# A two-layer decoder step: the sums of weights of the seven-product blocks made by adding transfers and VectorE, and the middle down products added up by transfers

## The chip, the cores and the metric

The kernel runs on one core of one Trainium2 chip. The metric is the time of one execution on the device, in microseconds (us). Before the change three runs gave 1215.65, 1221.56 and 1222.04 us, a median of 1221.56 us. The profile comes from one further execution of the same program.

## The reference, cut to what matters

One inference step runs a prompt of 512 tokens and 8 x 4 sample tokens, 544 rows in all, through two layers of width 1024. Layer 0 mixes tokens by causal pooling, layer 1 by a gated linear recurrence (HGRN2). Behind each mixer stands a gated ConvFFN, and the change lies in these two:

```python
def conv_ffn(h, ctx, w_up, conv_w, conv_b, w_down):
    L = h.shape[1]
    u = h @ w_up
    full = jnp.concatenate([ctx.astype(u.dtype), u], axis=1)
    c = conv_b + sum(full[:, j:j + L] * conv_w[j] for j in range(CONV_W))
    gate, val = jnp.split(c, 2, axis=-1)
    y = (jax.nn.gelu(gate, approximate=True) * val) @ w_down
    return y, full[:, -(CONV_W - 1):]
```

`w_up` is 1024 x 5632 (2816 gate and 2816 value columns), `w_down` 2816 x 1024, all float32.

## The kernel before, in words

**Layout.** Activations lie transposed: 128 channels on the partitions, 544 tokens along the free dimension. Each float32 operand of a large product is split into a rounded part and a remainder (`wh` and `wl` for weights, `h` and `l` for activations), and each product is three matmuls: `wh` by `h`, `wh` by `l`, `wl` by `h`. For a chunk of 128 x 512 weights ScalarE makes `wh` by copying, VectorE makes `wl` by subtracting (`ensure_units`). Ten buffers each for `wh` and `wl` let this run up to nine units ahead of TensorE (`ahead_units`).

**The ConvFFN (`ffn`).** The 2816 hidden channels are 22 pairs of one gate and one value block of 128. They come in five parts of 6, 4, 4, 3 and 5 pairs (`PARTS`). The down product of a part is eight blocks (`down(pi, o)`); those of part pi stand between the up products of part pi + 1 in the order of the table `MIX`, and the eight of the last part come at the end. `do_down` takes each result from its PSUM bank (`ps`) into the sum `m` (`mtile`): part 0 is copied by ScalarE, each later part is added by one VectorE instruction, `m<-m,ps`.

**Seven products instead of eight.** Pairs 0 to 5 are computed plainly. From pair 6 on, 16 pairs a layer, the gate and the value block are one 2 x 2 block product with seven half-size products in place of eight (`seven(j)`): the four halves of the two weight blocks and the two halves of the tokens are combined by sums and differences. The activations' sums are made once a layer in `operands(k, out)`, for k = 0 to 3, by four GpSimd subtractions of 128 x 272 each (tile `hold`, and `t`). The weights' sums are made for each pair in `seventh(i, q)`, q being the product: two loads of 512 KB fill two of the three `raw` buffers, three GpSimd additions of 128 x 512 follow, into a tile of its own (`sums`), into half of a `raw` buffer, and into a third tile (`fst`), and a fourth comes before the last product. A pair then takes 7 x 12 matmuls of 272 columns into three of the four PSUM banks called `pa`. ScalarE and VectorE combine the banks into `u`, and `finish` does the convolution: per block one ScalarE instruction (`t<-t,prm`), two VectorE instructions that multiply and add, SCALAR_TENSOR_TENSOR `t<-t,prm` 128x560, then for the gate a GELU on ScalarE, and for the pair the product `y` and its split into two parts for the down product.

**What sets the order.** Nearly every instruction is recorded by `Plan` and emitted by `Plan.emit`, a list scheduler that simulates the engines with the costs of `Plan.cost` and buffer release; the engines then run strictly in the emitted order. So a changed cost can move instructions anywhere in the program. Because a helper emits everything, all lines in the profile are L312, and tiles are what tells the groups apart.

**Names in the profile.** `raw`, `t`: loaded weights; `wup`, `wdn`: up and down weights in memory; `fst`: a tile that holds the convolution's saved rows and, behind them, a weight sum; `prm`: parameters; `op`, `k`, `xl`: split activations. The seven-product stages last from about 130 to 410 us in layer 0 and from about 880 to 1150 us in layer 1; `operands` runs at 80 to 130 and 830 to 880 us.

Of the kernel before, what the change touches and what calls it, by code (L numbers as in the profile page):

```python
# [17 lines left out]
P = 128  # L18
# [58 lines left out]
class Plan:  # L77
# [85 lines left out]
    @staticmethod  # L163
    def cost(eng, name, args, kw):
        out = args[0]
        n = 1
        for v in out.shape[1:]:
            n *= v
        if eng == "PE":
            f32 = str(args[1].dtype).endswith("float32")  # L170
            m = 1
            for v in args[1].shape[1:]:
                m *= v
            if name == "transpose":
                return 0.11
            if f32 and out.shape[0] <= 32 and args[1].shape[0] >= 96:
                return max(n / 2400 + 0.01, 0.0018 * m)
            return max(4 * n, 4 * min(m, 128)) / 2400 + 0.005 if f32 else n / 2400 + 0.003
        if name == "dma_start":
            return 0.475 if eng == "SP" else 1.04  # L180
        ins = [a for a in list(args[1:]) + list(kw.values()) if hasattr(a, "shape")]
        cols = sum(all(v == 1 for v in a.shape[1:]) for a in ins) if n > 1 else 0
        psum = any(str(getattr(a, "space", "")).endswith("PSUM") for a in ins)
        if eng == "ACT":
            return (0.0515 if psum else 0.0935) + n / 1200 + 0.0935 * cols
        if eng == "DVE":
            if name == "memset":
                return 0.01 + n / 960
            return 0.069 + n / (1920 if name == "tensor_scalar" and not psum else 960) + 0.06 * cols
        return 0.13 + n / 475  # L190

    def emit(self):
# [10 lines left out]
        dma = lambda o: 2.0 + int(np.prod(o[3][0].shape)) * 4 / 359e3  # L203
# [52 lines left out]
        for _ in range(n):  # L256
# [31 lines left out]
            if o[2] == "dma_start":  # L288
                st = max(at + o[7] + 0.65, dma_free)
                dma_free = st + dma(o) - 2.0  # L290
                end[i] = dma_free + 0.91
            else:
                end[i] = free[e]
# [52 lines left out]
def trunk_step(ctx: ExitStack, tc: _tile.TileContext, xT, xp, xs, spool, s0, fctx, par, gb0, cst, bands,  # L346
# [92 lines left out]
    sums, mine = {}, {}  # L439
# [39 lines left out]
    def seventh(i, q):  # L479


        H = 4 * P
        if q == 0:
            raws[i] = A_, B_ = [wp.tile([P, KT * P], F32, tag="raw", name="raw") for _ in range(2)]
            for t, src in zip((A_, B_), stream[i][0]):
                SP.dma_start(t, src)

            mine[i] = dict(sums) or {q: tt((P, H)) for q in range(2)}
            POOL.tensor_tensor(mine[i][0], A_[:, 0:H], B_[:, 0:H], op=ALU.add)
            POOL.tensor_tensor(B_[:, 0:H], B_[:, 0:H], B_[:, H:2 * H], op=ALU.add)  # L490
            POOL.tensor_tensor(mine[i][1], B_[:, 0:H], A_[:, 0:H], op=ALU.add)
        A_, B_ = raws[i]
        if q == 6:
            POOL.tensor_tensor(A_[:, H:2 * H], A_[:, H:2 * H], mine[i][1], op=ALU.add)
        return (mine[i][1], A_[:, 0:H], mine[i][0], B_[:, 0:H], A_[:, H:2 * H], B_[:, H:2 * H], A_[:, H:2 * H])[q]

# [415 lines left out]
    def ffn(li, XH, XL, res, enter, mtag, leave, n_ahead, homes, hv=HV):  # L912
# [70 lines left out]
        def do_down(pi, o, src, sl):  # L983
            if o == 0 and pi == LP and acc[0] is None:
                acc[0] = tt()
            if sl is None:
# [22 lines left out]
        def operands(k, out):  # L1009
# [22 lines left out]
        def operand(q, k):  # L1032

            t, c = ((out["a", k], 1), (out["a", k], 0), (out["w", k], 0), (out["w", k], 1), (out["z", k], 0), (out["s", k // 2], k % 2),
                    (out["z", k], 1))[q]
            return t[0][:, U[c]], t[1][:, U[c]]

        def seven(j):
            i = up_i[li, j]
            banks = [ps1()[:, 0:HT] for _ in range(3)]  # L1040
# [13 lines left out]
            Y, X, Z = banks  # L1054
            c, t = w[:, U[0]], w[:, U[1]]
            after = (lambda: ACT.activation(c, Y, AF.Identity),
                     lambda: DVE.tensor_tensor(t, c, X, op=ALU.subtract),
                     lambda: DVE.tensor_tensor(c, t, Z, op=ALU.add),
                     lambda: second(1, ALU.subtract, c, Y),
                     lambda: ACT.activation(u_of(0)[0][:, 2:2 + HT], X, AF.Identity),  # L1060
                     lambda: DVE.tensor_tensor(u_of(1)[0][:, 2:2 + HT], c, Z, op=ALU.add),
                     lambda: second(0, ALU.subtract, Y, t))
            for q, (o, more) in enumerate(((Y, 0), (X, 0), (Z, 0), (Y, 0), (X, 1), (Z, 0), (Y, 1))):
# [31 lines left out]
        def up(j):  # L1095
# [3 lines left out]
            for b in (j, NPAIR + j):  # L1099
# [3 lines left out]
                u, us = new_u(b)  # L1103
# [641 lines left out]
```

## Time and profile before

| What | Value |
|---|---|
| Runs | 1215.65, 1221.56, 1222.04 us, median 1221.56 |
| Profiled execution, its own time | 1218.57 us |
| Its span in the trace | 1216.7 us, 1.9 us less than its time |
| Granted TensorE clock over the span | 0.981 |
| TensorE busy | 1157.7 us (95%), 9892 matmuls |
| VectorE busy | 963.7 us (79%) |
| ScalarE busy | 632.7 us (52%) |
| GpSimd busy | 475.1 us (39%) |
| DMA | 134.04 MB, mean 110 GB/s |

A row of the groups gives line, engine, operation, written tile <- read tiles, shapes and count, then busy time and mean duration of one, then the idle time just before these instructions and what ended it. A row of the windows gives, for a stretch of the span, the busy time of each engine, the granted clock and the mean busy share of the 16 DMA engines. In a timeline row the first two numbers are start and duration; a bracket at the end is the engine's idle time before it and what ended that. DMA-issuing instructions on GpSimd do not count as busy.

### The profile page before, as it was taken

How to read it: one execution, taken by the hardware profiler on the slowest of the kernel's cores; microseconds unless marked ns; L12 is line 12 of the kernel's file. 1: busy time of each engine (PE TensorE's matmuls, PEld its weight loads, DVE VectorE, ACT ScalarE, POOL GpSimd, SP SyncE). 2: the span in 40 equal slices, each digit the busy share in tenths (PEclk: the TensorE clock that was granted, in tenths of full speed). 3: DMA queues.
4: the chain of work that ended last, by engine and by line, in shares of the span. 5: the costliest groups of instructions: out<-in, count | busy, mean ns of one | idle time of the engine just before them, and what ended most of it. 6: DMA issues, size and time to landing. Idle time of an engine off the chain costs nothing.

```text
span 1216.7 us, 25725 instructions
## 1 busy us (share of the span) xinstructions
PE 1157.7 (95%) x9892; PEld 1116.1 (92%) x9892; DVE 963.7 (79%) x2075; ACT 632.7 (52%) x1343; POOL 475.1 (39%) x709
## 2 busy tenths in 40 slices
PE   8999898999999999999999999999899999999895
PEld 7799898998999997999999999999899899998895
DVE  6788776888988877588778985577976998888866
ACT  4665555444444466556555554545545544444552
POOL 3547535354454233111111130427625446355413
PEclk9999999999999999999999999999899999999998
DMA  9883232221321376423232223457141232223232
GB/s 322 188 206 73 61 109 88 88 87 61 113 96 65 110 247 142 105 82 108 92 105 84 83 98 117 119 141 157 40 139 71 71 104 96 78 83 96 63 142 74
DMA packets 55243, 134.04 MB, mean 110 GB/s; under 512 B 6730, under 2 KB 13258, under 8 KB 55112
## 3 DMA queue, kind: packets, MB, share of 16 engines
q1 hardware_dynamic: 37168, 95.90, 23.4%
q0 software_dynamic: 17808, 36.44, 13.0%
q8 instruction: 78, 1.28, 0.4%
q14 instruction: 45, 0.37, 0.1%
q10 hardware_dynamic: 144, 0.05, 0.0%
HBM read 119.96 MB, written 12.77 MB: 109 GB/s over the span
## 4 chain that ended last, share of the span: by engine, by line
PE 58%; DVE 23%; issue 7%; ACT 6%; POOL 4%; DMA 2%; DVEq 0%; SPq 0%; ACTq 0%; POOLq 0%
PE ps L312 30%; PE pa L312 27%; DVE t L312 13%; DVE wl L312 5%; ACT t L312 3%; DVE m L312 2%; ACT wh L312 2%; PE pr L312 2%; POOL raw L312 1%; POOL fst L312 1%; DMA t<-bands 1%; DVE k L312 1%; DVE op L312 1%; POOL wh L312 0%; DMA k<-wup 0%
## 5 line engine op out<-in xcount | busy, mean ns | idle before, releaser
L312 PE MATMUL pa<-op,wh 128*128 128x272 f32 x1152 | 268.8, 298 | 23.6 <-ACT t L312 15.6
L312 ACT ACTIVATE wh<-raw 128x512 fp32r<-128x512 f32 (+2 forms) x294 | 172.7, 597 | 168.6 <-PE ps L312 68.0
L312 PE MATMUL ps<-t,wh 128*128 128x272 f32 x1248 | 241.3, 291 | 6.1 <-ACT t L312 4.2
L312 DVE TENSOR_TENSOR wl<-raw,wh 128x512 fp32r<-128x512 f32 (+2 forms) x294 | 199.5, 691 | 59.4 <-ACT wh L312 53.1
L312 PEld LDWEIGHTS pa<-op,wh 128*128 128x128 f32 x1152 | 200.3, 195 | 29.5 <-ACT t L312 18.9
L312 PE MATMUL pa<-op,wl 128*128 128x272 f32 x768 | 226.3, 295 | 0.9 <-DVE wl L312 0.9
L312 DVE SCALAR_TENSOR_TENSOR t<-t,prm 128x560 f32<-128x560 f32 (+1 forms) x184 | 191.3, 1071 | 22.5 <-ACT t L312 21.7
L312 PEld LDWEIGHTS ps<-t,wh 128*128 128x128 f32 x1248 | 198.1, 190 | 8.2 <-ACT t L312 5.1
L312 DVE TENSOR_TENSOR t<-t 128x512 f32<-128x512 f32 (+10 forms) x332 | 154.3, 487 | 36.4 <-ACT t L312 28.0
L312 PE MATMUL ps<-t,wl 128*128 128x272 f32 x624 | 180.2, 290 | 1.6 <-DVE wl L312 1.6
L312 POOL COPY fst<-t 128x2 f32<-128x2 f32 (+1 forms) x176 | 82.8, 554 | 248.9 <-DVE t L312 248.8
L312 PE MATMUL ps<-xh,wh 128*128 128x256 f32 (+1 forms) x560 | 166.4, 298 | 0.0
L312 ACT ACTIVATE t<-t 128x544 fp32r<-128x544 f32 (+5 forms) x145 | 85.2, 598 | 155.1 <-DVE t L312 152.7
L312 PE MATMUL ps<-xl,wh 128*128 128x256 f32 (+1 forms) x560 | 162.3, 290 | 0.5 <-DVE xl L312 0.5
L312 PE MATMUL ps<-xh,wl 128*128 128x256 f32 (+1 forms) x560 | 160.9, 288 | 0.4 <-DMA wl<-wup 0.4
L312 PEld LDWEIGHTS pa<-op,wl 128*128 128x128 f32 x768 | 149.6, 195 | 1.1 <-DVE wl L312 1.1
L312 PE MATMUL pa<-k,wh 128*128 128x272 f32 (+2 forms) x560 | 139.5, 293 | 4.6 <-ACT k L312 3.4
L312 PEld LDWEIGHTS ps<-t,wl 128*128 128x128 f32 x624 | 118.6, 190 | 2.0 <-DVE wl L312 2.0
L312 PEld LDWEIGHTS ps<-xh,wh 128*128 128x128 f32 x560 | 105.4, 188 | 3.8 <-issue 1.6
L312 PEld LDWEIGHTS ps<-xl,wh 128*128 128x128 f32 x560 | 105.5, 188 | 3.7 <-issue 2.0
L312 PEld LDWEIGHTS ps<-xh,wl 128*128 128x128 f32 x560 | 105.3, 188 | 2.7 <-issue 1.8
L312 PEld LDWEIGHTS pa<-k,wh 128*128 128x128 f32 x560 | 99.4, 192 | 5.4 <-ACT k L312 3.6
(207 smaller groups left out, 2472.7 us busy)
## 6 DMA issues: line engine op xcount, KB each, us to landing
raw<-wup SPq DMA_DIRECT2D x69, 512.0 KB, 3.3
raw<-win SPq DMA_DIRECT2D x26, 512.0 KB, 3.3
wh<-wup POOLq DMA_DIRECT2D x34, 256.0 KB, 5.4
wl<-wup POOLq DMA_DIRECT2D x34, 256.0 KB, 5.0
t<-wdn SPq DMA_DIRECT2D x32, 256.0 KB, 4.1
raw<-wdn SPq DMA_DIRECT2D x16, 384.0 KB, 3.0
raw<-wdn SPq DMA_DIRECT2D x16, 320.0 KB, 4.4
yT<-x SPq DMA_DIRECT2D x16, 272.0 KB, 6.2
```

The source lines that it names most:

```text
L312: o[1](*o[3], **o[4])
```

## The change

1. **Weight sums.** The seven products use another set of sums. In `seventh` SyncE loads half of the second block (`w1`) into a half of a `raw` buffer, and a GpSimd-issued transfer adds the other half of `w1` on top in place (`accum_op=ALU.add`). The same is done with the first half of `w0` and the second of `w1` in the buffer's other half. The first block is loaded whole (512 KB) into a second `raw` buffer, and one half of `w1` once more into a tile of its own (`sums` or `fst`, by turns). Two VectorE additions of 128 x 512, `raw<-raw`, come before products 2 and 5. The four GpSimd additions are gone.
2. **Four banks.** `seven` takes four `pa` banks instead of three, and its steps of combining are reordered to fit.
3. **Buffers taken later.** `new_u` gets a bank: the GpSimd memset and copy that open `u` now wait until TensorE has written that bank.
4. **Middle down products.** For parts 1 to 3, `do_down` copies the bank to a tile `t` by ScalarE, and a GpSimd-issued transfer adds that tile to `m`. The last part is still added by VectorE.
5. **Activation sums.** The four subtractions in `operands` move from GpSimd to VectorE, and `operand` picks another order of halves.
6. **The planner's costs.** A GpSimd-issued transfer costs 0.9 in place of 1.04, an adding one 1.75 times the time per byte, the landing on GpSimd's queue 2.4, a GpSimd copy 0.55, a small memset 0.19.

```diff
@@ cost, emit
-            return 0.475 if eng == "SP" else 1.04
+            return 0.475 if eng == "SP" else 0.9
...
-        dma = lambda o: 2.0 + int(np.prod(o[3][0].shape)) * 4 / 359e3
+        dma = lambda o: 2.0 + int(np.prod(o[3][0].shape)) * 4 / 359e3 * (1.75 if "accum_op" in o[4] else 1)
...
-                end[i] = dma_free + 0.91
+                end[i] = dma_free + (2.4 if e == "POOL" else 0.91)
@@ def seventh(i, q):
         H = 4 * P
+        lo, hi = slice(0, H), slice(H, 2 * H)
+        w0, w1 = stream[i][0]
         if q == 0:
-            raws[i] = A_, B_ = [wp.tile([P, KT * P], F32, tag="raw", name="raw") for _ in range(2)]
-            for t, src in zip((A_, B_), stream[i][0]):
-                SP.dma_start(t, src)
-
-            mine[i] = dict(sums) or {q: tt((P, H)) for q in range(2)}
-            POOL.tensor_tensor(mine[i][0], A_[:, 0:H], B_[:, 0:H], op=ALU.add)
-            POOL.tensor_tensor(B_[:, 0:H], B_[:, 0:H], B_[:, H:2 * H], op=ALU.add)
-            POOL.tensor_tensor(mine[i][1], B_[:, 0:H], A_[:, 0:H], op=ALU.add)
-        A_, B_ = raws[i]
-        if q == 6:
-            POOL.tensor_tensor(A_[:, H:2 * H], A_[:, H:2 * H], mine[i][1], op=ALU.add)
-        return (mine[i][1], A_[:, 0:H], mine[i][0], B_[:, 0:H], A_[:, H:2 * H], B_[:, H:2 * H], A_[:, H:2 * H])[q]
+            B_, A_ = [wp.tile([P, KT * P], F32, tag="raw", name="raw") for _ in range(2)]
+            raws[i] = A_, B_, sums[i % 2] if sums else tt((P, H))
+            SP.dma_start(B_[:, hi], w1[:, lo])
+            POOL.dma_start(B_[:, hi], w1[:, hi], accum_op=ALU.add)
+            SP.dma_start(A_, w0)
+            SP.dma_start(B_[:, lo], w0[:, lo])
+            POOL.dma_start(B_[:, lo], w1[:, lo], accum_op=ALU.add)
+            SP.dma_start(raws[i][2], w1[:, hi])
+        A_, B_, C_ = raws[i]
+        if q in (2, 5):
+            DVE.tensor_tensor(B_[:, hi], B_[:, hi], A_[:, lo if q == 2 else hi], op=ALU.add)
+        return (A_[:, lo], B_[:, hi], B_[:, hi], B_[:, lo], A_[:, hi], B_[:, hi], C_)[q]
@@ def new_u(j, bank=None):
+            if bank is not None:
+                plan.after(bank)
             POOL.memset(u[:, 0:2], 0.0)
+            if bank is not None:
+                plan.after(bank)
             POOL.tensor_copy(us[:, :, 0:2], cv[:, j])
@@ def do_down(pi, o, src, sl):
+            if pi < LP:
+
+                e = tt()
+                ACT.activation(whole(e, ps)[0], src, AF.Identity)
+                POOL.dma_start(mtile[:, o, :], e, accum_op=ALU.add)
+                return
             DVE.tensor_tensor(m, m, src, op=ALU.add)
-            if pi < LP:
-                return
@@ def operands(k, out):
-            POOL.tensor_tensor(w[:, U[0]], za[:, U[1]], zb[:, U[1]], op=ALU.subtract)
...
+            DVE.tensor_tensor(w[:, U[0]], za[:, U[1]], zb[:, U[1]], op=ALU.subtract)
...
@@ def seven(j):
-            banks = [ps1()[:, 0:HT] for _ in range(3)]
+            banks = [ps1()[:, 0:HT] for _ in range(4)]
...
-            for q, (o, more) in enumerate(((Y, 0), (X, 0), (Z, 0), (Y, 0), (X, 1), (Z, 0), (Y, 1))):
+            for q, (o, more) in enumerate(((X, 0), (Y, 0), (W, 0), (Z, 0), (X, 1), (Y, 1), (Z, 1))):
```

How the emitted order changes is shown on two engines at one place, the pairs of the last part (part 4) in layer 0, where each pair is followed by two down blocks of part 3 (128x384 weights). First GpSimd, before, from one pair's last weight sum to the next pair's sums:

```order
L312 TENSOR_TENSOR raw<-raw,fst 128x512
L312 COPY fst<-t 128x16
L312 COPY fst<-t 128x2
L312 TENSOR_TENSOR sums<-raw 128x512
L312 TENSOR_TENSOR raw<-raw 128x512
L312 TENSOR_TENSOR fst<-raw 128x512
L312 COPY fst<-t 128x2
```

And now, over one pair, where `raw<-wup` are the two adding weight transfers and `m<-t` the additions of down blocks:

```order
L314 DMA raw<-wup 128x512 x2
L314 DMA m<-t 128x544 x2
L314 COPY t<-fst 128x8x2
L314 MEMSET t 128x2
L314 COPY fst<-t 128x2
L314 COPY t<-fst 128x8x2
L314 MEMSET t 128x2
L314 COPY fst<-t 128x16
```

GpSimd's four additions are gone from the place, and issues of four adding transfers stand there, ahead of the opening of the pair's own `u` tiles (`t<-fst`, MEMSET), which before stood elsewhere.

Second VectorE in the same stretch, before, from the first convolution step to the splitting of the next weights:

```order
L312 SCALAR_TENSOR_TENSOR t<-t,prm 128x560
L312 TENSOR_TENSOR m<-m,ps 128x544
L312 SCALAR_TENSOR_TENSOR t<-t,prm 128x560 x2
L312 TENSOR_TENSOR m<-m,ps 128x544
L312 SCALAR_TENSOR_TENSOR t<-t,prm 128x560
L312 TENSOR_TENSOR t<-t 128x512
L312 TENSOR_TENSOR t<-t 128x32
L312 TENSOR_TENSOR wl<-t,wh 128x384 x2
L312 TENSOR_TENSOR wl<-fst,wh 128x512
```

And now:

```order
L314 SCALAR_TENSOR_TENSOR t<-t,prm 128x560
L314 TENSOR_TENSOR wl<-t,wh 128x384
L314 SCALAR_TENSOR_TENSOR t<-t,prm 128x560 x2
L314 TENSOR_TENSOR wl<-t,wh 128x384
L314 SCALAR_TENSOR_TENSOR t<-t,prm 128x560
L314 TENSOR_TENSOR t<-t 128x512
L314 TENSOR_TENSOR wl<-raw,wh 128x512
L314 TENSOR_TENSOR t<-t 128x32
L314 TENSOR_TENSOR wl<-raw,wh 128x512
L314 TENSOR_TENSOR raw<-raw 128x512
L314 TENSOR_TENSOR t<-t 128x544
```

The two `m<-m,ps` between the convolution's steps are gone, the splitting of the down weights stands in their places, and the new addition `raw<-raw` stands behind the second weight split, ahead of the split of `y` (`t<-t` 128x544).

More of the change, by code (lines that the diff above doesn't have):

```diff
@@ L189, in cost @@
             return 0.069 + n / (1920 if name == "tensor_scalar" and not psum else 960) + 0.06 * cols
-        return 0.13 + n / 475
+        if name == "tensor_copy":
+            return 0.55
+        return 0.19 if name == "memset" and n < 99 else 0.13 + n / 475
     def emit(self):
@@ L438, in trunk_step @@
     raws, casts = {}, {}
-    sums, mine = {}, {}
+    sums = {}
     def ensure(upto):
@@ L926, in cw, with new_u @@
             return pcol(O_CW + (li * 3 + tap) * 44 + j)
-        def new_u(j):
+        def new_u(j, bank=None):
             u = tt((P, UW))
@@ L985, in do_down @@
                 acc[0] = tt()
+            ps = src
             if sl is None:
@@ L1015, in operands @@
                 SP.dma_start(yT[:, f], x_of(f))
-            POOL.tensor_tensor(w[:, U[0]], za[:, U[1]], zb[:, U[1]], op=ALU.subtract)
-            POOL.tensor_tensor(w[:, U[1]], za[:, U[0]], za[:, U[1]], op=ALU.subtract)
-            POOL.tensor_tensor(za[:, U[1]], za[:, U[0]], w[:, U[0]], op=ALU.subtract)
-            POOL.tensor_tensor(s_, zb[:, U[0]], za[:, U[1]], op=ALU.subtract)
+            DVE.tensor_tensor(w[:, U[0]], za[:, U[1]], zb[:, U[1]], op=ALU.subtract)
+            DVE.tensor_tensor(w[:, U[1]], za[:, U[0]], za[:, U[1]], op=ALU.subtract)
+            DVE.tensor_tensor(za[:, U[1]], za[:, U[0]], w[:, U[0]], op=ALU.subtract)
+            DVE.tensor_tensor(s_, zb[:, U[0]], za[:, U[1]], op=ALU.subtract)
             both(out["a", k], za)
@@ L1032, in operand @@
         def operand(q, k):
-            t, c = ((out["a", k], 1), (out["a", k], 0), (out["w", k], 0), (out["w", k], 1), (out["z", k], 0), (out["s", k // 2], k % 2),
-                    (out["z", k], 1))[q]
+            t, c = ((out["a", k], 0), (out["w", k], 1), (out["a", k], 1), (out["w", k], 0), (out["z", k], 0),
+                    (out["z", k], 1), (out["s", k // 2], k % 2))[q]
             return t[0][:, U[c]], t[1][:, U[c]]
@@ L1045, in u_of @@
                 if o not in us_:
-                    us_[o] = new_u(o * NPAIR + j)
+                    us_[o] = new_u(o * NPAIR + j, X)
                 return us_[o]
@@ L1053, in second @@
                                   b[:, n1:HT].rearrange("p (b t) -> p b t", t=NL), op=op)
-            Y, X, Z = banks
+            X, Y, W, Z = banks
             c, t = w[:, U[0]], w[:, U[1]]
[L1056 to L1059, printed above, removed]
+            after = (lambda: ACT.activation(c, X, AF.Identity),
+                     lambda: None,
+                     lambda: (DVE.tensor_tensor(t, W, c, op=ALU.subtract), DVE.tensor_tensor(c, t, Y, op=ALU.subtract)),
+                     lambda: second(1, ALU.add, c, Z),
                      lambda: ACT.activation(u_of(0)[0][:, 2:2 + HT], X, AF.Identity),
-                     lambda: DVE.tensor_tensor(u_of(1)[0][:, 2:2 + HT], c, Z, op=ALU.add),
-                     lambda: second(0, ALU.subtract, Y, t))
-            for q, (o, more) in enumerate(((Y, 0), (X, 0), (Z, 0), (Y, 0), (X, 1), (Z, 0), (Y, 1))):
+                     lambda: second(0, ALU.subtract, Y, t),
+                     lambda: DVE.tensor_tensor(u_of(1)[0][:, 2:2 + HT], t, Z, op=ALU.add))
+            for q, (o, more) in enumerate(((X, 0), (Y, 0), (W, 0), (Z, 0), (X, 1), (Y, 1), (Z, 1))):
                 ahead_units(unit0[i] + q)
@@ L1102, in up @@
                 t = block(i, rH, rL, KT, HP)
-                u, us = new_u(b)
+                u, us = new_u(b, None if li == 0 and j < 8 else t[:, 0, 0:HP])
                 evac_full(u, us, t)
```

## The prediction

> **What bounds the kernel now.** I read first the windows, cut at the stages that the change touches. Columns: stretch, its length, busy time of TensorE, its weight loads, VectorE, ScalarE and GpSimd (instructions in brackets), granted clock, DMA share, GB/s.
>
> ```profile
> 80.00:130.00 50.00, 46.29 (x362) 45.86 (x362) 44.78 (x68) 28.81 (x47) 35.99 (x59) 0.99 0.44 95
> 130.00:188.00 58.00, 57.74 (x449) 57.15 (x448) 39.22 (x73) 29.07 (x54) 22.61 (x37) 0.98 0.29 92
> 188.00:410.00 222.00, 207.72 (x1565) 204.29 (x1564) 191.96 (x313) 106.21 (x189) 102.97 (x141) 0.96 0.25 84
> 830.00:880.00 50.00, 45.34 (x340) 44.63 (x339) 45.18 (x63) 29.46 (x49) 35.69 (x51) 0.93 0.40 87
> 880.00:930.00 50.00, 49.53 (x393) 49.12 (x392) 33.84 (x61) 23.50 (x43) 17.35 (x21) 1.00 0.34 106
> 930.00:1150.00 220.00, 205.88 (x1569) 201.75 (x1569) 190.12 (x307) 105.17 (x189) 109.56 (x152) 0.98 0.25 84
> ```
>
> TensorE is the bound, and its work does not change. What can be won is its idle time and the clock lost behind it. In the two long seven-product stretches it idles 222 - 207.7 = 14.3 and 220 - 205.9 = 14.1 us, together 28.4; the clock takes (1 - 0.96) x 222 = 8.9 and (1 - 0.98) x 220 = 4.4, together 13.3. Where the activation sums are made (80 to 130, 830 to 880) idle is 3.7 + 4.7 = 8.4 and clock 0.5 + 3.5 = 4.0. The idle follows VectorE: at 68% VectorE (130 to 188, 880 to 930) TensorE idles 0.3 us of 58 and 0.5 of 50, at 86% it idles 6%.
>
> Then the timelines around one long gap, which show how VectorE comes to be late. VectorE:
>
> ```profile
> 361.48 1.50 DVE L312 SCALAR_TENSOR_TENSOR t<-t,prm 128x560 f32<-128x560 f32 x1 [0.99 <-ACT t L312]
> 362.89 0.71 DVE L312 TENSOR_TENSOR m<-m,ps 128x544 f32<-128x544 f32 x1
> 363.52 2.95 DVE L312 SCALAR_TENSOR_TENSOR t<-t,prm 128x560 f32<-128x560 f32 x2
> 366.39 0.71 DVE L312 TENSOR_TENSOR m<-m,ps 128x544 f32<-128x544 f32 x1
> 367.02 0.79 DVE L312 SCALAR_TENSOR_TENSOR t<-t,prm 128x560 f32<-128x560 f32 x1
> ```
>
> GpSimd, with three weight sums:
>
> ```profile
> 361.08 1.29 POOL L312 TENSOR_TENSOR sums<-raw 128x512 f32<-128x512 f32 x1 [0.30 <-DMA raw<-wup]
> 362.45 1.67 POOL L312 TENSOR_TENSOR raw<-raw 128x512 f32<-128x512 f32 x1
> 364.20 1.67 POOL L312 TENSOR_TENSOR fst<-raw 128x512 f32<-128x512 f32 x1
> ```
>
> ScalarE:
>
> ```profile
> 366.50 0.67 ACT L312 ACTIVATE t<-t 128x560 f32<-128x560 f32 x1 [4.32 <-DVE t L312]
> ...
> 369.47 0.37 ACT L312 ACTIVATE t<-pa 128x272 f32<-128x272 f32 x1
> ```
>
> And TensorE:
>
> ```profile
> 369.89 0.51 PE L312 MATMUL pa<-op,wh 128*128 128x272 f32 x2 [2.20 <-ACT t L312]
> ```
>
> The same multiply-and-add takes 1.50 us, and 2.95 for two, while GpSimd adds, and 0.79 once GpSimd is done. The additions from PSUM, `m<-m,ps`, take 0.71 both times. So only instructions with both tensors in SBUF are stretched. ScalarE stands 4.32 us idle at the GELU that waits for them; the copy that frees a bank is queued behind it, and TensorE waits 2.20 us for that copy. The waits over the whole span (total, times, longest) name the same releaser for TensorE, and a second one, the activation sums (`op`), behind GpSimd's `hold`:
>
> ```profile
> PE pa L312 <- ACT t L312: 16.0, 12, 2.2
> ...
> ACT op L312 <- POOL hold L312: 7.9, 6, 2.8
> ...
> PE pa L312 <- ACT op L312: 3.7, 1, 3.7
> ```
>
> **The change part by part.** Groups of before, with their shapes kept apart, last columns busy time, mean ns:
>
> ```profile
> L312 DVE TENSOR_TENSOR wl<-raw,wh 128x512 fp32r<-128x512 f32 x262 | 188.1, 729 | 56.2 <-ACT wh L312 50.0 <-PE pa L312 5.1
> L312 DVE SCALAR_TENSOR_TENSOR t<-t,prm 128x560 f32<-128x560 f32 x176 | 185.0, 1084 | 21.3 <-ACT t L312 20.8
> L312 DVE TENSOR_TENSOR m<-m,ps 128x544 f32<-128x544 f32 x56 | 39.4, 710 | 9.1 <-PE ps L312 9.1
> L312 DVE TENSOR_TENSOR t<-t 128x512 f32<-128x512 f32 x44 | 36.9, 839 | 6.4 <-ACT t L312 4.0 <-POOL fst L312 0.5 <-ACT wh L312 0.5
> L312 POOL DMA_DIRECT2D wl<-wup x34 | 30.6, 981 | 21.3 <-ACT wl L312 21.2
> L312 DVE TENSOR_TENSOR wl<-sums,wh 128x512 fp32r<-128x512 f32 x30 | 20.5, 682 | 0.1
> L312 DVE TENSOR_TENSOR t<-t 128x272 f32<-128x272 f32 x40 | 17.8, 445 | 2.3 <-PE pa L312 2.0 <-ACT q L312 0.3
> L312 ACT ACTIVATE m<-ps 128x544 f32<-128x544 f32 x16 | 9.9, 616 | 16.0 <-PE ps L312 16.0
> ```
>
> *Weight sums off GpSimd.* The stretch goes with the additions: 176 x (1.084 - 0.79) = 51.7 us on the multiply-and-adds, 262 x (0.729 - 0.682) = 12.3 on the weight splits (`wl<-sums` is the unstretched row of that form), 44 x (0.839 - 0.682) = 6.9 on the products `y`, together 71 us of VectorE. The two new `raw<-raw` additions a pair cost 64 x 0.682 = 43.6 us, taken from that same form. Here a rule of the Trainium skill is to be weighed. The three additions above last 1.29 + 1.67 + 1.67 = 4.63 us, and what they put on VectorE is 1.50 - 0.79 + 2.95 - 2 x 0.79 = 2.1 us. The Trainium skill, SBUF — State Buffer, section Who interferes with whom, says that a VectorE instruction with two SBUF inputs and a GpSimd instruction that reads SBUF exclude each other for the whole instruction. By that rule 128 additions of about 1.54 us would give back 198 us instead of 71, and the forecast would move to the lower end of the range; the trace shows less than half of it, and I go by the rows.
>
> *Middle down products.* 48 of the 56 `m<-m,ps` leave VectorE: 48 x 0.710 = 34.1 us. ScalarE gets 48 copies of that form from PSUM, 48 x 0.616 = 29.6 us, and the adding transfers follow. Nobody waits for those soon: the next part's addition to the same block of `m` is a part later.
>
> *Activation sums.* 32 subtractions of 128 x 272 come to VectorE, 32 x 0.445 = 14.2 us, and leave GpSimd, where the 3.7 us wait begins: TensorE waits for ScalarE's `op`, and that for GpSimd's `hold`.
>
> VectorE in all: -71 - 34.1 + 43.6 + 14.2 = -47 us. In the seven-product stages alone: -71 - 34.1 + 43.6 = -61.5 of 39.2 + 192.0 + 33.8 + 190.1 = 455 us, so from 83% of 550 us to 76% of 520. ScalarE there goes from 264 us (48%) to 294 (56%). Both stay below the bound.
>
> *Four banks, buffers taken later.* A bank of a pair is used again by the next pair only after two products or more of cover, about as before: nothing either way. The memset and copy of `u` now wait for TensorE on GpSimd, and the adding transfers of `m` and of the next weights are queued behind. GpSimd loses 128 additions and gets 112 issues of 0.98 us (the `wl<-wup` row), so it has room; bounds 0 to 2 us, from none to one late issue in each part; I take 0.
>
> *The transfers.* These rows price them:
>
> ```profile
> q1 hardware_dynamic: 37168, 95.90, 23.4%
> q0 software_dynamic: 17808, 36.44, 13.0%
> ```
>
> ```profile
> raw<-wup SPq DMA_DIRECT2D x69, 512.0 KB, 3.3
> wl<-wup POOLq DMA_DIRECT2D x34, 256.0 KB, 5.0
> raw<-wdn SPq DMA_DIRECT2D x16, 320.0 KB, 4.4
> t<-pw SPq DMA_DIRECT2D x4, 256.0 KB, 9.7
> wl<-win POOLq DMA_DIRECT2D x12, 256.0 KB, 5.9
> ```
>
> Plain loads move 95.90 MB in 23.4% of 1216.7 = 284.7 us, 0.337 MB per us, so 256 KB take 0.78 us of all 16 engines. On q0 46 adding transfers (`wl`, 12.06 MB) share 158.2 us with 24.38 MB of plain ones; at the plain rate these take 72.3, which leaves 85.9 us, 1.87 us per adding 256 KB at most. A pair then needs 5 x 0.78 + 2 x 1.87 = 7.6 us in place of 3.1, a middle down block 2.0 us more. That is 32 x 4.5 + 48 x 2.0 = 240 us more in the stages, on top of 0.29 x 58 + 0.25 x 222 + 0.34 x 50 + 0.25 x 220 = 144: a share of 384 / 520 = 74%. Not full, but landings get longer: the bounds are 3.3 us (today) and 9.7 us (`pw`, in the crowded first 80 us); I take 5, near the 4.4 of `wdn`, which is loaded where the share is 0.63:
>
> ```profile
> 410.00:440.00 30.00, 30.00 (x242) 30.00 (x241) 21.82 (x46) 17.34 (x34) 5.97 (x13) 1.00 0.63 222
> ```
>
> The half-summed buffer is loaded a pair ahead, so its 3.3 + 5.0 us and more lie beside 11 us of matmuls (84 x 205.88 / 1569 us). The other buffer waits for one to come free; see the rivals. I take 2 us for all late landings.
>
> **The sum.** The stretch cost 2.1 us at the gap shown, and two `m<-m,ps` of 0.71 stood in the same run: 3.5 us against a gap of 2.2. So gaps of this kind should close, but at 76% VectorE lies midway between the stages that hardly idle (68%) and those that do (86%), and what is late next is ScalarE's queue and the chain addition, copy, split. I let a third stay, my choice: saved are 2/3 x 28.4 = 18.9 of idle and 2/3 x 13.3 = 8.9 of clock. At the activation sums, where VectorE gains work, I take a third: 1/3 x (8.4 + 4.0) = 4.1. With the 2 us for landings that is 18.9 + 8.9 + 4.1 - 2 = 29.9 us. The profiled execution took 1218.6 us, 0.2% below the median of the runs, 1221.6: 1218.6 - 29.9 = 1188.7, so 1189. If all of it went, 1218.6 - 28.4 - 13.3 - 12.4 = 1164.5; if a third, 1218.6 - 1/3 x 41.7 = 1204.7.
>
> **The rivals.**
>
> *The wait moves to ScalarE (1205).* ScalarE runs in order and gets 29.6 us of copies, and its weight copies now wait for `raw<-raw` on VectorE. For it: the longest entry of TensorE's waits names ScalarE. Against: ScalarE's idle of 4.32 us there was itself a wait for VectorE. Only a third comes back: 1204.7.
>
> *Nothing to measure (1216).* If the gaps come from ScalarE's order and not from the stretch, the saving is eaten by the 29.6 us of copies, of which a tenth on the path leaves 1216 to 1222. Against it speaks the gap shown.
>
> *The second buffer's load is late (1241, slower).* Three `raw` buffers serve two a pair, so the 512 KB of a pair start when the previous pair's last addition frees a buffer. From there to the next such addition lie the landing and, at best, addition, copy, split, addition: 3 x 0.68 + 0.62 = 2.7 us; at worst, all that VectorE does for a pair, (455 - 61.5) / 32 = 12.3 us. A pair with its down blocks has 520 / 32 = 16.3 us. So it decides from a landing between 4.0 and 13.6 us, midway about 9. The Trainium skill, DMA: Bandwidth & Descriptors, section Issuing engines are not separate DMA queues, says that all queues end in the same 16 engines and interleave; that speaks for it. At 11 us, 2 us late on 26 pairs (the first three of each layer start early), 52 us come in: 1188.7 + 52 = 1241. Against: the 5 us above.
>
> **How the numbers follow.** A difference under 0.5% (6 us) can't be told from none here. Forecast (1165 to 1204) 0.62, a third 0.20, nothing 0.09, late load 0.09. The range of 1166 to 1212 leaves out the last two and the edge of the forecast. Faster: 0.62 + 0.20 = 0.82; same 0.09; slower 0.09.
>
> **What would show it.** Right: multiply-and-adds near 0.79 us in the mean, VectorE about 47 us less busy, TensorE idle of some 10 us in the two stretches together and a clock near 0.99, a DMA share of about 0.7. Wrong: `ACT wh` or `DVE raw` waiting for `DMA raw` for tens of us and a landing of `raw<-wup` of 9 us or more (late load); or TensorE idle as before with short multiply-and-adds (ScalarE).

## The result, and the profile after

| Kernel | Runs | Median us | Lowest to highest |
|---|---|---|---|
| before, beside it | 4 | 1218.61 | 1215.43 to 1222.04 |
| after | 4 | 1168.63 | 1168.05 to 1170.23 |

The ratio is 0.9591, with a 95% interval of 0.9555 to 0.9628: 50 us faster. The forecast was 1189, the range 1166 to 1212: the time lies 20 us below the forecast, 3 us inside the range's lower end. The profiled execution took 1168.88 us.

The page of after: span, busy times, the DMA queue q0 (packets, MB, share) and the chain that ended last.

```profile
span 1167.1 us, 26141 instructions
...
PE 1145.6 (98%) x9896; PEld 1105.2 (95%) x9896; DVE 906.5 (78%) x2123; ACT 667.1 (57%) x1391; POOL 361.7 (31%) x661
...
q0 software_dynamic: 33936, 66.60, 28.9%
...
PE 93%; DVE 4%; DMA 1%; ACT 1%; issue 0%; SPq 0%; DVEq 0%; ACTq 0%
```

The span fell by 1216.7 - 1167.1 = 49.6 us. TensorE's idle time fell from 1216.7 - 1157.7 = 59.0 to 21.5 us, which is 37.5 of it; its busy time fell from 1157.7 to 1145.6, which is the other 12.1, at a granted clock of 0.994 in place of 0.981. The chain of before was TensorE for 58%, VectorE for 23%; now it is TensorE for 93%. Before:

```profile
PE 58%; DVE 23%; issue 7%; ACT 6%; POOL 4%; DMA 2%; DVEq 0%; SPq 0%; ACTq 0%; POOLq 0%
```

The windows of after, with the columns of the prediction's first fence; each stage starts a little earlier in layer 1:

```profile
80.00:130.00 50.00, 50.00 (x399) 50.00 (x398) 47.46 (x96) 31.60 (x50) 23.86 (x40) 1.00 0.53 111
130.00:188.00 58.00, 58.00 (x464) 58.00 (x464) 44.48 (x87) 33.27 (x62) 14.30 (x28) 1.00 0.53 137
188.00:410.00 222.00, 222.00 (x1770) 222.00 (x1769) 183.73 (x356) 136.40 (x239) 80.12 (x160) 1.00 0.72 183
800.00:850.00 50.00, 50.00 (x396) 50.00 (x395) 46.46 (x92) 32.47 (x53) 32.86 (x56) 1.00 0.57 130
850.00:900.00 50.00, 50.00 (x401) 50.00 (x400) 36.72 (x70) 27.18 (x50) 9.14 (x22) 1.00 0.54 142
900.00:1110.00 210.00, 210.00 (x1675) 210.00 (x1674) 173.63 (x326) 128.60 (x224) 77.10 (x153) 1.00 0.69 167
```

Busy time equals the stretch in every row, and the clock is 1.00: in the stages of the change neither idle time nor lost clock is left. VectorE is at 83% of the two long stretches, hardly less than the 86% of before, and TensorE does not wait for it.

The groups of after that answer to those of the prediction (last columns: busy time, mean ns, idle before):

```profile
L314 DVE TENSOR_TENSOR wl<-raw,wh 128x512 fp32r<-128x512 f32 x294 | 202.0, 696 | 85.5 <-ACT wh L314 78.9 <-PE pa L314 4.4
L314 DVE SCALAR_TENSOR_TENSOR t<-t,prm 128x560 f32<-128x560 f32 x176 | 134.9, 796 | 2.3 <-ACT t L314 1.8
L314 DVE TENSOR_TENSOR raw<-raw 128x512 f32<-128x512 f32 x64 | 43.9, 686 | 0.6
L314 DVE TENSOR_TENSOR t<-t 128x512 f32<-128x512 f32 x44 | 30.2, 686 | 3.3 <-ACT t L314 2.1
L314 DVE TENSOR_TENSOR m<-m,ps 128x544 f32<-128x544 f32 x8 | 5.6, 715 | 4.8 <-PE ps L314 4.8
```

The multiply-and-adds went from 1.084 to 0.796 us, while the additions from PSUM, 0.710 before, still take 0.715: what was stretched is what reads two tensors from SBUF.

Waits (total, times, longest), the first row of before and the others of after, and then the DMA issues of after (count, KB, median us to landing):

```profile
ACT t L312 <- DVE t L312: 207.5, 107, 6.6
...
ACT t L314 <- DVE t L314: 67.2, 73, 4.8
...
ACT wh L314 <- DMA raw<-wup: 4.4, 5, 1.5
```

```profile
raw<-wup SPq DMA_DIRECT2D x37, 512.0 KB, 3.2
raw<-wup SPq DMA_DIRECT2D x64, 256.0 KB, 3.6
raw<-wup POOLq DMA_DIRECT2D x64, 256.0 KB, 5.8
m<-t POOLq DMA_DIRECT2D x48, 272.0 KB, 6.0
```

ScalarE's wait for VectorE fell from 207.5 us (107 times) to 67.2. GpSimd waits a good deal now, 60.1 us for loads of up weights and 61.6 for ScalarE's copies, but ScalarE waits only 0.8 us for GpSimd. ScalarE waits only 4.4 us for up weights in `raw`.

### The profile page after: what moved, and what is told of

Its sections match the earlier page's. It is cut to its first block, busy times and chain, and to the rows that moved or that the text cites. A ratio compares the mean times of both kernels' runs of the same rounds, so it can differ in the third digit from the quotient of the medians.

```text
span 1167.1 us, 26141 instructions
## 1 busy us (share of the span) xinstructions
PE 1145.6 (98%) x9896; PEld 1105.2 (95%) x9896; DVE 906.5 (78%) x2123; ACT 667.1 (57%) x1391; POOL 361.7 (31%) x661
## 4 chain that ended last, share of the span: by engine, by line
PE 93%; DVE 4%; DMA 1%; ACT 1%; issue 0%; SPq 0%; DVEq 0%; ACTq 0%
PE pa L314 46%; PE ps L314 44%; PE pr L314 3%; DVE t L314 2%; DVE m L314 1%; DMA t<-bands 1%; ACT t L314 1%; DVE o L314 0%; DVE wl L314 0%; DVE x L314 0%; DVE c L314 0%; DVE Al L314 0%; SPq L314 0%; DVE q L314 0%; DVE Asp L314 0%
## 5 line engine op out<-in xcount | busy, mean ns | idle before, releaser
L314 ACT ACTIVATE wh<-raw 128x512 fp32r<-128x512 f32 x326 | 192.9, 603 | 182.9 <-PE ps L314 69.0
L314 DVE TENSOR_TENSOR wl<-raw,wh 128x512 fp32r<-128x512 f32 x326 | 212.3, 662 | 87.5 <-ACT wh L314 80.9
L314 PE MATMUL pa<-op,wh 128*128 128x272 f32 x1152 | 255.8, 288 | 0.0
L314 PE MATMUL ps<-t,wh 128*128 128x272 f32 x1248 | 236.6, 288 | 0.0
L314 PE MATMUL pa<-op,wl 128*128 128x272 f32 x768 | 221.4, 288 | 0.0
L314 PEld LDWEIGHTS pa<-op,wh 128*128 128x128 f32 x1152 | 193.0, 188 | 0.0
L314 POOL COPY fst<-t 128x16 f32<-128x16 f32 (+1 forms) x176 | 91.1, 565 | 251.1 <-DVE t L314 250.8
L314 DVE TENSOR_TENSOR t<-t 128x512 f32<-128x512 f32 (+9 forms) x332 | 141.4, 449 | 30.8 <-ACT t L314 23.7
L314 PEld LDWEIGHTS pa<-op,wl 128*128 128x128 f32 x768 | 144.6, 188 | 0.0
L314 DVE SCALAR_TENSOR_TENSOR t<-t,prm 128x560 f32<-128x560 f32 (+1 forms) x184 | 141.1, 796 | 3.6 <-ACT t L314 2.9
```

The source lines that it names most:

```text
L314: o[1](*o[3], **o[4])
```

## The experiments

Three theories were on the table at first. S: the gain is the end of the stretch, and the rest of the change weighs little. Its rivals were that VectorE's work counts, whatever its kind (W), and that the order counts: banks, opening, recalibrated costs (O). After eight runs the opening of `u` had turned out to be large, and two explanations of that were set against each other. B: an opened `u` holds one of the 22 tiles `t`, and the middle down products need such tiles for their copies. P: early opening costs by itself, down transfers or not.

| Kernel | Median us (lowest to highest) | Ratio to before, 95% interval |
|---|---|---|
| e1_down_vec | 1172.33 (1171.24 to 1172.89) | 0.9596, 0.9559 to 0.9632 |
| e2_gps_add | 1177.72 (1175.67 to 1179.99) | 0.9641, 0.9601 to 0.9682 |
| e3_old_costs | 1161.21 (1160.64 to 1162.07) | 0.9506, 0.9470 to 0.9542 |
| e4_only_down | 1240.12 (1236.52 to 1242.78) | 1.0142, 1.0093 to 1.0190 |
| e5_sums_vec | 1207.21 (1206.35 to 1207.63) | 0.9890, 0.9874 to 0.9906 |
| e6_not_later | 1210.64 (1208.40 to 1211.22) | 0.9916, 0.9897 to 0.9934 |
| e7_ops_gps | 1176.83 (1174.11 to 1177.36) | 0.9637, 0.9619 to 0.9656 |
| e8_double | 1181.18 (1178.26 to 1186.95) | 0.9679, 0.9639 to 0.9719 |
| e9_neither | 1191.98 (1190.59 to 1193.40) | 0.9778, 0.9740 to 0.9817 |
| e10_t21 | 1166.97 (1166.60 to 1167.49) | 0.9577, 0.9546 to 0.9608 |
| e11_later_only | 1197.14 (1195.01 to 1197.79) | 0.9822, 0.9789 to 0.9855 |
| e12_down_later | 1204.33 (1200.79 to 1205.81) | 0.9879, 0.9843 to 0.9916 |

The medians of before beside them are 1220.35 (e1 to e4), 1221.45 (e5 to e8) and 1217.27 us (e9 to e12); beside after it was 1218.61. So a difference between kernels of different groups, after included, is uncertain by some 4 us. Each edit also lets the planner make another order: a time holds the part and the order together, while busy times and mean durations say what the part itself does.

### The stretch: e5, e2, e7

**e5_sums_vec** is the kernel before, with the four additions of each pair's weights on VectorE:

```diff
-            POOL.tensor_tensor(mine[i][0], A_[:, 0:H], B_[:, 0:H], op=ALU.add)
+            DVE.tensor_tensor(mine[i][0], A_[:, 0:H], B_[:, 0:H], op=ALU.add)
...
-            POOL.tensor_tensor(A_[:, H:2 * H], A_[:, H:2 * H], mine[i][1], op=ALU.add)
+            DVE.tensor_tensor(A_[:, H:2 * H], A_[:, H:2 * H], mine[i][1], op=ALU.add)
```

> The kernel before, with its four weight additions a pair on VectorE in place of GpSimd and nothing else: VectorE gets 128 x 0.68 = 87 us more work of its own and loses the stretch of 71 us. Theory S: VectorE's busy time stays about the same (964 + 16 = 980 us), so the time stays near, 1205 to 1230 us, although GpSimd does nothing there any more. Rival W: 87 us more on an engine that is 86% busy in these stages, 1250 us or more.

It is 14 us faster than the kernel before although VectorE has 128 additions more, some 87 us of work. Its busy times and its groups:

```profile
PE 1150.0 (95%) x9892; PEld 1112.9 (92%) x9892; DVE 978.5 (81%) x2203; ACT 634.1 (53%) x1343; POOL 288.5 (24%) x581
```

```profile
L312 DVE TENSOR_TENSOR wl<-raw,wh 128x512 fp32r<-128x512 f32 x262 | 177.1, 689 | 32.4 <-ACT wh L312 26.1 <-PE pa L312 5.1
L312 DVE SCALAR_TENSOR_TENSOR t<-t,prm 128x560 f32<-128x560 f32 x176 | 140.5, 825 | 11.4 <-ACT t L312 11.0
```

VectorE's busy time rises by only 978.5 - 963.7 = 14.8 us, so the 87 us of additions took some 72 us of stretch away. W expected the opposite sign. The stretch is shown, by itself, in the kernel before. The 14 us are not the stretch's alone: in before ScalarE also waits 38.0 us for GpSimd's sums in `raw`, and that goes with them.

**e2_gps_add** is after, with its two `raw<-raw` additions a pair on GpSimd.

```diff
-            DVE.tensor_tensor(B_[:, hi], B_[:, hi], A_[:, lo if q == 2 else hi], op=ALU.add)
+            POOL.tensor_tensor(B_[:, hi], B_[:, hi], A_[:, lo if q == 2 else hi], op=ALU.add)
```

> The changed kernel, but the two additions of 128 x 512 a pair stand on GpSimd in place of VectorE: VectorE has 44 us less to do, GpSimd adds beside it again, half as often as before. Theory S: the multiply-and-adds go from 0.80 to about 0.93 us, half of the old stretch of 71 us returns, idle of TensorE returns, 1178 to 1195 us. Rival W: VectorE has less work, so 1167 to 1170 us. Rival O: as W.

```profile
L314 DVE TENSOR_TENSOR wl<-raw,wh 128x512 fp32r<-128x512 f32 x294 | 227.5, 788 | 82.6 <-ACT wh L314 77.0 <-PE pa L314 4.3
L314 DVE SCALAR_TENSOR_TENSOR t<-t,prm 128x560 f32<-128x560 f32 x176 | 140.5, 829 | 3.5 <-POOL t L314 1.2 <-ACT t L314 0.7 <-issue 0.2
L314 POOL TENSOR_TENSOR raw<-raw 128x512 f32<-128x512 f32 x64 | 98.9, 1546 | 64.9 <-DVE wl L314 57.4 <-ACT t L314 5.8 <-DVE lbm L314 1.3
```

It loses 9 us (6 by the ratios, whose intervals overlap). VectorE gave away 43.9 us of work and is 917.0 us busy, 10.5 more than in after: 64 additions of 1.546 us stretched it by 54 us. The multiply-and-adds take 0.829 us and not the 0.93 expected. The stretch falls on whatever runs beside it: in before mostly on the multiply-and-adds, here mostly on the weight splits (696 to 788 ns).

**e7_ops_gps** is after, with the four subtractions of `operands` back on GpSimd (`DVE.` to `POOL.` in each).

```diff
-            DVE.tensor_tensor(w[:, U[0]], za[:, U[1]], zb[:, U[1]], op=ALU.subtract)
+            POOL.tensor_tensor(w[:, U[0]], za[:, U[1]], zb[:, U[1]], op=ALU.subtract)
...
```

> The changed kernel, but the subtractions for the activation sums stand on GpSimd again (14 us off VectorE, 36 us on GpSimd, at 80 to 130 us and 800 to 850 us). Theory S: the stretch and the wait for them return in these two stages, of the 12.4 us of idle and clock there a half to all: 1174 to 1182 us. Rival W: 1165 to 1169 us.

It loses 8 us (6 by the ratios, whose intervals overlap), and idle time returns where the sums are made: 2.27 us at 121, 0.89 at 139, 2.12 at 826. For the two long ones the trace names no releaser.

### Opening and down products: e1, e6, e4, and then e9, e11, e12, e10

**e1_down_vec** is after, with all down products added by VectorE again.

```diff
-            if pi < LP:
-
-                e = tt()
-                ACT.activation(whole(e, ps)[0], src, AF.Identity)
-                POOL.dma_start(mtile[:, o, :], e, accum_op=ALU.add)
-                return
             DVE.tensor_tensor(m, m, src, op=ALU.add)
+            if pi < LP:
+                return
```

> The changed kernel, but the middle down products are added by VectorE from PSUM again (48 instructions of 0.71 us, 34 us more for VectorE; ScalarE loses 30 us). Theory S (the gain is the stretch of VectorE beside GpSimd's additions, which stays away here): 1168 to 1176 us, multiply-and-adds still 0.80 us. Rival W (the gain is VectorE having less work of its own): 34 of its 57 us come back, so about 1169 + 0.6 x 50 = 1199 us, at least 1190. Rival O (the order of the instructions): close to 1169.

VectorE is at 932.4 us, 26 more, and the kernel only 3.7 us slower, less than the uncertainty between the groups: the down transfers are worth next to nothing here.

**e4_only_down** is before with that part alone.

```diff
+            ps = src
...
+            if pi < LP:
+                e = tt()
+                ACT.activation(whole(e, ps)[0], src, AF.Identity)
+                POOL.dma_start(mtile[:, o, :], e, accum_op=ALU.add)
+                return
             DVE.tensor_tensor(m, m, src, op=ALU.add)
-            if pi < LP:
-                return
```

> The kernel before, with only the middle down products added by transfers: VectorE loses 34 us of its own work, the stretch beside GpSimd's additions stays. Theory S: multiply-and-adds still near 1.05 us, a third of the gain at most, 1203 to 1219 us. Rival W: 34 of 57 us, about 30 us faster, 1185 to 1195 us. Rival O: 1219 us.

All theories missed: it is 20 us slower. The multiply-and-adds stay at 1084 ns, and TensorE gets new gaps, the longest in the two long stretches 4.4 us. Where they come from, in its waits and on ScalarE:

```profile
PE ps L312 <- ACT t L312: 25.7, 11, 4.4
...
242.25 0.66 ACT L312 ACTIVATE t<-t 128x544 fp32r<-128x544 f32 x1 [3.99 <-DVE t L312]
242.81 1.12 ACT L312 ACTIVATE t<-ps 128x544 f32<-128x544 f32 x2
```

The new copies of the banks (`t<-ps`) stand on ScalarE behind the split of `y`, and that waits 3.99 us for VectorE, while GpSimd adds. TensorE waits for the banks, 25.7 us in all, where before it was 4.2. So the wait moved to ScalarE, as one of the prediction's rivals had it. ScalarE waits only 3.4 us for down weights here, and no load on SyncE waits for an adding transfer.

**e6_not_later** is after, with `u` opened early as before.

```diff
-                    us_[o] = new_u(o * NPAIR + j, X)
+                    us_[o] = new_u(o * NPAIR + j)
...
-                u, us = new_u(b, None if li == 0 and j < 8 else t[:, 0, 0:HP])
+                u, us = new_u(b)
```

> The changed kernel, but the memset and copy that open u no longer wait for the bank. Theories S and W: no difference, 1166 to 1172 us. Rival O: part of the gain goes, 1175 us or more.

It loses 42 of the 50 us, with short multiply-and-adds (796 ns); S and W had expected no difference. Its windows, and three of its waits:

```profile
188.00:410.00 222.00, 208.61 (x1600) 205.80 (x1599) 160.32 (x315) 118.98 (x209) 69.20 (x149) 0.97 0.62 151
...
930.00:1150.00 220.00, 209.10 (x1622) 206.35 (x1621) 163.93 (x313) 119.39 (x211) 70.81 (x149) 0.98 0.62 153
```

```profile
ACT wh L314 <- DMA t<-wdn: 27.2, 15, 3.9
...
PE ps L314 <- ACT wh L314: 10.9, 6, 3.3
...
SPq L314 <- DMA m<-t: 38.5, 6, 9.1
```

TensorE idles 13.4 and 10.9 us there, about as in before, while VectorE is at only 72% and 75%. ScalarE now waits 27.2 us for down weights (`t<-wdn`), and TensorE for ScalarE's splits of them. SyncE stands 38.5 us, six times, until an adding transfer `m<-t` has landed, each time just before it loads down weights: there the load waits for a tile `t` that the transfer holds. One load and one split of this kernel, and then of after:

```profile
351.56 1.44 SPq L314 DMA_DIRECT2D t<-wdn  x1
...
357.13 0.53 ACT L314 ACTIVATE wh<-t 128x384 fp32r<-128x384 f32 x1 [1.27 <-DMA t<-wdn]
```

```profile
340.73 0.83 SPq L314 DMA_DIRECT2D t<-wdn  x2
...
355.48 0.52 ACT L314 ACTIVATE wh<-t 128x384 fp32r<-128x384 f32 x1
```

With early opening the weights are asked for some 5 us ahead of their split, and they take 5.0 us to land (4.9 in after); in after they are asked for some 15 us ahead. Down weights are loaded into tiles `t`, of which there are 22, and an opened `u` holds tiles of the same pool. Over all 48 loads and all 88 openings, each paired in order of time (the load counted from the end of its issue):

| Kernel | `u` opened early | downs by transfer | load issued ahead of its split, median us | opening ahead of the convolution, median us | median time |
|---|---|---|---|---|---|
| before | yes | no | 6.4 | 64.9 | 1218.6 |
| e4_only_down | yes | yes | 6.0 | 65.8 | 1240.1 |
| e11_later_only | no | no | 16.6 | 8.7 | 1197.1 |
| e12_down_later | no | yes | 16.2 | 7.1 | 1204.3 |
| e9_neither (rest as after) | yes | no | 5.1 | 64.7 | 1192.0 |
| e6_not_later (rest as after) | yes | yes | 5.1 | 65.3 | 1210.6 |
| e1_down_vec (rest as after) | no | no | 15.0 | 10.2 | 1172.3 |
| after | no | yes | 14.8 | 7.8 | 1168.6 |

Three of these kernels were made to complete the squares. **e9_neither** joins the edits of e1 and e6, **e11_later_only** is before with the later opening alone, **e12_down_later** joins that with e4:

```diff
-        def new_u(j):
+        def new_u(j, bank=None):
...
+            if bank is not None:
+                plan.after(bank)
             POOL.memset(u[:, 0:2], 0.0)
...
-                    us_[o] = new_u(o * NPAIR + j)
+                    us_[o] = new_u(o * NPAIR + j, X)
```

> The changed kernel without two of its parts: u is opened early again, and the middle down products are added by VectorE. Without the later opening alone the time was 1211 us, with the down products on VectorE alone 1172. Theory B (buffers: there are 22 of the tiles t; a down block added by a transfer holds one until it has landed, u tiles that are opened early hold others, and the loads of down weights find none): with no such tiles the early opening costs little, 1172 to 1182 us. Rival P (the later opening is worth its 42 us by itself): 1205 to 1215 us.

> The kernel before with only the later opening of u (memset and copy wait for the bank). Theory B: there no transfer holds a tile, so little changes, 1205 to 1222 us. Rival P: most of the 42 us, 1180 to 1195 us.

> The kernel before with the middle down products added by transfers (alone 1240 us) and the later opening of u. Theory B: the later opening gives the tiles that the transfers hold, the 20 us come back and some of VectorE's relief shows, 1200 to 1218 us, a gain against the opening alone or none, but no loss. Rival P: 1240 - 42 = 1198 us and as much below the later opening alone as 1240 is above 1220, that is 20 us slower than the later opening alone.

In both squares the later opening is worth 20 us without down transfers (1218.6 to 1197.1, 1192.0 to 1172.3) and 36 to 42 with them. Down transfers with early opening cost 19 to 22 us in both; with later opening they lose 7 in before and are worth nothing clear in after (3.7 us). So P is right that early opening costs by itself, and B that the down transfers make it worse; neither alone gives the numbers.

The lead of the loads goes with the opening in all eight kernels, but it is not what TensorE waits for in all of them. In before ScalarE waits for no down weights in `t` at all, in e4 3.4 us, in e9 8.3, in e6 27.2; of the 48 splits, 2 start within 0.4 us of the landing in before, 6 in e4, 17 in e9 and 20 in e6. So late down weights are a path to TensorE in e6 and hardly elsewhere. What early opening costs by itself is seen in two waits of TensorE in e9, six gaps of 16.8 us together that e1 does not have, where the idle times of the two differ by 19.2 us:

```profile
PE ps L314 <- DVE wl L314: 8.7, 2, 5.3
PE pa L314 <- ACT t L314: 8.1, 4, 4.4
```

In the first the weight split stands on VectorE behind multiply-and-adds, in the longest of the second ScalarE's copy of a bank stands behind the GELU and the split of `y`. Both are in e6 too. The second is also the picture of before in the prediction. e11 shows what becomes of it there, and it separates opening and stretch: its stretch is all there (1132 ns), and yet it is 20 us faster. Its group, one of its waits (16.0 us in before), and ScalarE at the like place:

```profile
L312 DVE SCALAR_TENSOR_TENSOR t<-t,prm 128x560 f32<-128x560 f32 x176 | 195.3, 1132 | 12.4 <-ACT t L312 9.1 <-POOL fst L312 1.5 <-POOL raw L312 1.1
...
PE pa L312 <- ACT t L312: 3.5, 7, 0.9
...
357.37 0.40 ACT L312 ACTIVATE t<-pa 128x272 f32<-128x272 f32 x1 [2.58 <-PE pa L312]
...
360.82 0.66 ACT L312 ACTIVATE t<-t 128x560 f32<-128x560 f32 x1
```

The bank's copy now stands ahead of the GELU (the last row), so the late multiply-and-adds no longer hold it up. Part of that goes to waits for VectorE itself, 12.1 us against 2.9: in all TensorE's idle time falls from 59.0 to 45.0 us and its busy time by 6.7. That this order is the whole of the 20 us is not shown.

**e10_t21** is after with one tile `t` less.

```diff
-    tp = ctx.enter_context(tc.tile_pool(name="tp", bufs=22))
+    tp = ctx.enter_context(tc.tile_pool(name="tp", bufs=21))
```

> The changed kernel with 21 tiles t in place of 22, nothing else. Theory B: buffers are what limits it, so one less costs a good part of the 42 us, 1175 to 1190 us. Rival P: 1167 to 1171 us.

No loss (1166.97 us). With late opening there is room for a tile less; this speaks neither for nor against a shortage when `u` is opened early. A pool larger or much smaller was not tried. So what is shown is that the opening costs, through the order of the instructions by itself, and through tiles that loads wait for once down transfers use the pool too (e6). Why the planner makes the worse order when `u` is opened early, and whether more tiles would mend it, stays open.

### The loads: e8

**e8_double** is after, with each pair's 512 KB block loaded twice.

```diff
             SP.dma_start(A_, w0)
+            SP.dma_start(A_, w0)
```

> The changed kernel, but the whole first weight block (512 KB) of each pair is loaded twice in a row into its buffer, so that the load that starts when a buffer comes free takes about 2 us longer or more and the DMA share rises by about 0.1. If the late-load rival lies just behind the edge: 2 us on 26 pairs, about 1220 us. If landing has the slack that the prediction gave it (about 4 us): 1168 to 1175 us.

It loses 12.5 us, between the two expectations. The median landing of one such transfer is 4.6 us in place of 3.2, but SyncE's timeline shows that the second load of the block waits for the first:

```profile
339.18 2.26 SPq L314 DMA_DIRECT2D raw<-wup  x3
...
342.97 0.33 SPq L314 DMA_DIRECT2D raw<-wup  x1
```

Over the 32 pairs it is issued 3.1 to 7.0 us behind the first, 4.1 in the median. So the block is there 4.1 + 4.6 = 8.7 us after it is first asked for, and that is the landing that this kernel tries. ScalarE's wait for these loads grows from 4.4 to 41.9 us, and part of it reaches TensorE:

```profile
ACT wh L314 <- DMA raw<-wup: 41.9, 23, 5.5
...
PE pa L314 <- ACT wh L314: 7.1, 4, 3.0
```

So at about 9 us late loads begin to cost, and little as yet. The second load also holds up what stands behind it on SyncE, down weights among it; the two are not told apart.

### The planner's costs: e3

**e3_old_costs** is after with `Plan.cost` and the landing times of before.

```diff
-            return 0.475 if eng == "SP" else 0.9
+            return 0.475 if eng == "SP" else 1.04
...
-                end[i] = dma_free + (2.4 if e == "POOL" else 0.91)
+                end[i] = dma_free + 0.91
```

> The changed kernel with the planner's costs of before (adding transfers as cheap as plain ones, landing early, small GpSimd instructions cheaper), so another order with the same work. Rival O (the gain is the order): 1190 us or more. Theories S and W: the work and the stretch are those of the change, 1168 to 1180 us, with some waits for adding transfers that the order takes for landed.

It is the fastest kernel of all, 7.4 us ahead of after, outside both expectations, and the intervals of the two ratios do not touch. The recalibrated costs are no part of the gain (O); they take something off it. TensorE's idle time is the same, 21.4 against 21.5 us; its busy time is 7.1 us less, at the same granted clock of 0.994. Where: the first and last start of the seven-product matmuls, per layer, in after and then in e3:

```profile
L314 PE MATMUL pa<-op,wh x448: 282/288/293, 130.7 to 400.2; 128*128 128x272 f32 x150
L314 PE MATMUL pa<-op,wh x704: 282/288/293, 847.1 to 1117.8; 128*128 128x272 f32 x176
```

```profile
L312 PE MATMUL pa<-op,wh x448: 282/288/395, 126.9 to 397.5; 128*128 128x272 f32 x150
L312 PE MATMUL pa<-op,wh x704: 282/288/293, 839.9 to 1110.4; 128*128 128x272 f32 x176
```

e3 is 3.8 us ahead when the first of them starts, 2.7 when those of layer 0 end, 7.2 when those of layer 1 start and 7.4 at their end. All of it is won outside the seven-product stages, ahead of 130 us and between the layers. What in the order there does it was not settled.

## Why the prediction was right, and where its sizes were off

**The bound and the stretch: right.** TensorE was the bound, and its idle time is what went. By size: multiply-and-adds 185.0 - 134.9 = 50.1 us (forecast 51.7), weight splits 262 x (0.729 - 0.696) = 8.6 (12.3), products `y` 6.7 (6.9), added `raw<-raw` 43.9 (43.6), down products 33.8 (34.1). VectorE fell by 57.2 us and not by 47, since forms I had not counted were stretched too (among them eight `op<-hold,op` from 1056 to 718 ns, 52 small `t<-t` of 128 x 32 from 255 to 185). e5 and e2 showed the mechanism from both sides. The rule of the Trainium skill that I weighed (SBUF — State Buffer, Who interferes with whom: exclusion for the whole instruction) again goes too far in size: in e2, 98.9 us of GpSimd additions put 54 us on VectorE. Its direction holds.

**"Four banks, buffers taken later ... I take 0": the main miss.** I had weighed what the later opening queues on GpSimd, and not what it does to the order on the other engines. e11 shows 20 us for it in the kernel before, e6 42 in after. The gaps of before thus had two causes, as far as the waits show, VectorE's stretch and an order in which the bank's copy stands on ScalarE behind what the stretch delays; I had seen both in one gap, and put the second down to the first. Late down weights are no cause there: ScalarE does not wait for them. I had also read the idle time off VectorE's share (68% hardly any, 86% some): after idles nothing at 83%, and e6 6% at 72%. The share was a sign beside the cause. The four banks were not tried apart.

**"Middle down products": a saving in the wrong place.** The 33.8 us left VectorE as forecast, and were worth 3.7 us at most (e1). Without the later opening they cost about 20 (e4, e6 against e9), for which the sum had no term. In e4 the copies stand on ScalarE behind an instruction that waits for VectorE. In e6 each copy holds a tile `t` until its transfer has landed, and loads of down weights wait for it (38.5 us).

**"I let a third stay": nothing stayed.** In the six windows no idle time is left, and TensorE's idle fell by 37.5 us over the span. I had put the lost clock at 17.3 us in all, of which the sum took 10.2; TensorE's busy time fell by 12.1. For the activation sums I had taken a third of 12.4 us; e7 puts that part alone at 6 to 8.

**The transfers.** q0 grew by 30.16 MB and by 0.289 x 1167.1 - 158.2 = 179 us of the 16 engines, so an adding 256 KB takes 1.56 us in the mean of both kinds, within the bound of 1.87 (by the same sum 1.70 in e1, where only weights are added). The share of 0.72 and 0.69 is near the 0.74. Landings of the plain loads stayed at 3.2 and 3.6 us, below the 5 I took, and the 2 us for late ones did not come. I had put the point from which the late load decides at about 9 us; e8, with its block there after 8.7, loses 12.5 us, which fits.

**The planner's costs** had no price in the sum; e3 puts them at 7 us against the change.

By steps, e9, e1 and after give the path of the gain: 1218.6 to 1192.0 for weight sums, banks, activation sums and costs together, to 1172.3 with the later opening, to 1168.6 with the down transfers. That the stretch's part (27 us with all that comes beside it) lies near my 30 is chance: my sum had the right cause for half of the gain, and no term for the other half. Without the later opening the change as I priced it comes to 1210.6 (e6), at the range's other end.

## What to carry to other kernels

Where a planner makes the order, the start of an instruction on an idle engine is an edit to the whole program: here 88 tiles opened 65 us ahead cost 20 to 42 us. Look in the trace for what stands ahead of a bank's copy, and for loads that wait until another user gives back a tile. A relief of an engine that is not the bound is worth what its wait was worth, so look at the wait after each part of a change, not at the busy time. Tuned costs of a planner are an edit like any other: run them alone.

## What the runs showed of the hardware

Small GpSimd instructions get long right behind a DMA that GpSimd issues. In after, the 48 memsets that open a `u` within 2.5 us of such an issue take 587 ns in the mean, the other 40 take 95. GpSimd's timeline of after, at two places (start, duration):

```profile
346.34 0.88 POOL L314 DMA_DIRECT2D m<-t  x1 [0.94 <-ACT t L314]
346.88 0.93 POOL L314 COPY t<-fst 128x16 f32<-128x16 f32 x1
347.01 0.83 POOL L314 MEMSET t<- 128x2 f32 x1
...
352.85 0.19 POOL L314 COPY t<-fst 128x16 f32<-128x16 f32 x1
352.98 0.09 POOL L314 MEMSET t<- 128x2 f32 x1
```

The same copy takes 0.19 or 0.93 us, the memset 0.09 or 0.83. In the mean the memset takes 125 ns in before and 122 in e11, 222 with 48 adding transfers more than before (e12), 353 with 64 (e1) and 363 with 112 (after). Whether it works or waits in that time the trace does not say.

An adding transfer of 256 KB takes 1.56 us of the 16 engines against 0.78 for a plain one, and 5.8 us to land; a plain one of that size takes 3.6 when SyncE issues it (`raw<-wup`) and 4.3 when GpSimd does (`wh<-wup`). The 112 issues on GpSimd did not stretch VectorE as its additions had: the multiply-and-adds take 796 ns beside them, and 799 in e1, where there are 64.
